# A fixed instruction order for TensorE in two chunked recurrences

## The chip, the core and the metric

The kernel runs on one core of one Trainium2 chip. The metric is the device time of one execution in microseconds; the profile beside it is that of one execution on the chip. TensorE (PE) multiplies matrices into PSUM, VectorE (DVE), ScalarE (ACT) and GpSimd (POOL) do the elementwise work, SyncE (SP) issues transfers.

## What is computed

One layer of a streaming encoder: a normalised and modulated input `h`, one input projection, two recurrences side by side (GLA with 4 heads of 64 x 128, HGRN2 with 4 heads of 128 x 128), a gated norm, and an output projection with a residual. 4096 prompt frames and 64 sample frames, width 1024. The recurrence of each head is

```
S_t = diag(exp g_t) S_{t-1} + k_t^T v_t,    o_t = q_t S_t
```

```python
h = rms_norm(x, g_pre) * (1 + scale[:, None]) + shift[:, None]
p = jnp.einsum('btd,de->bte', h, w_in)
q_a, k_a, v_a, z_a, a_lr, q_h, f_h, i_h, z_h = jnp.split(p, ...)
o_a, s_a = chunked_gla(q_a * GLA_DK ** -0.5, k_a, v_a, log_alpha, s_gla)
o_h, s_h = chunked_gla(silu(q_h), 1 - f, i_h, log(f), s_hgrn)
...
y = x + gate[:, None] * rms_norm(o, g_post)
```

Any evaluation of the recurrence that gives these values will do; the chunk size is free.

## The kernel before

The prompt is cut into 16 groups of 256 tokens (two tiles of 128); the 64 sample tokens ride as a third tile with the last group in GLA and with group 2 in HGRN. The kernel walks over the groups three times: GLA, HGRN, and a last pass with the output projection. Each projection is split into a high and a low part, three matmuls for each product.

**Main and sides.** In both recurrences a group's projection is a generator (`proj_gla`, `proj_hgrn`), and `weave` runs other generators beside it. The projection yields after every four and eight of its eight contraction steps (`proj_feat`, features by tokens, 12 matmuls of 256 columns a half; `proj_tok`, tokens by features, 12 matmuls of 264 or 512 columns a half). At each yield `weave` takes as many steps of each side as are due. Sides are: the `attend` of the group before, the preparation of the next group's input (`prep_x` in GLA, `prep_h` in HGRN), weights, and `gate_rows`. For a side `(gen, n, first, last)`, n steps are spread evenly over the yields `first` to `last`. A GLA group has 20 yields (four features of q and k, four z blocks, two v tiles), an HGRN group 20 as well (four f and four q features, two tiles of i).

**The order on the engines.** What the program traces is not yet the order in which an engine runs. A planner orders each engine's instructions with modelled times, by the order of the program as a priority and by what is ready; it also places tiles in the pools' buffers and adds every wait. TensorE's order is therefore the planner's. Only the first group's setup (`first_group`) stands in a block that keeps program order.

**The steps of an attend** (line 642), as `attend` yields. The first is taken right after the projection (`next(side)`), the other twelve beside the next group's projection:
1. nothing
2. transposes of A (L686), sums and products on VectorE
3. half as many transposes of A
4. transposes of A again
5. the first Y, and 6. the second Y (`prepare`, L911)
7. and 8. the score matmuls L956 on the Y's, `place` (L923) and `times`. GLA has two pairs of blocks, both in step 7; HGRN has four, two in step 7 and two in step 8
9. and 10. the levels 5 and 6 (L766)
11. and 12. the chunks: keys transposed (L793), A times v (L818), Q times S (L823), the state's increment (L839), the state's update (L850), the norm

The score part of `three_levels` (line 884), with pr running over the pairs of blocks:

```python
        ys = [prepare(0)]
        yield
        if NP > 1:
            ys.append(prepare(1))
        yield
        for pr in range(NP):
            ...
            Yt = ys.pop(0)
            ...
            if pr + 2 < NP:
                ys.append(prepare(pr + 2))
            if pr % 2 or pr == NP - 1:
                ...
```

Between `Yt = ys.pop(0)` and the next `prepare` stand the matmuls L956 of one pair (16 records in HGRN, 32 in GLA), which read Yt and K. `prepare` takes a tile from the pool `wstage`, which has two buffers: a whole one (`stage_pair`) for 128-token chunks, a half of one (`wst`, which cuts a pair and keeps the unused half in `self.halves`) for the 64-token set. Weights are staged in halves of the same pool. A Y is filled by a memset on GpSimd (L915), a copy on ScalarE (L916) and six products on VectorE, each of which reads the one before (L909).

**The input's norm in GLA.** From group 2 on, `quad_norm` (line 502) takes eight squares on ScalarE (L514), a small matmul with `same` (L517), a root, and a product; `x_turn` (line 522) transposes x on VectorE in four steps, modulates it into `hf`, and stores `hf` to `h_d`, where HGRN reads it again. `split_h` splits `hf` into the two parts `hh` that the next projection reads.

Of the kernel before, what the change touches and what calls it, by code (L numbers as in the profile page):

```python
# [15 lines left out]
P = 128  # L16
# [6 lines left out]
C_QA, C_VA, C_ZA, C_AL, C_QH, C_FH, C_IH, C_ZH = 0, 512, 1024, 1536, 1552, 2064, 2576, 3088  # L23
NMASK = 8
END = 20
LEVELS = 1


class Kernel:
# [472 lines left out]
    def quad_norm(self, g, js):  # L502

        nc = self.nc
        ss = self.small.tile([P, 8], F32, name="q_ss")
        n = 0
        tiles = []
        for j in js:
            nb = self.groups[g][j][2] // 32
            xv = self.xs[j][:, : nb * 256].rearrange("p (b f) -> p b f", b=nb)  # L510
            tiles.append((xv, n, nb))
            for b in range(nb):
                junk = self.ap.tile([P, 256], mybir.dt.bfloat16, name="sqx", bufs=1)
                nc.scalar.activation(junk, xv[:, b], AF.Square, accum_out=ss[:, n : n + 1])  # L514
                n += 1
        pt = self.ps("tp")[:, :n]
        nc.tensor.matmul(pt, self.same, ss[:, :n], start=True, stop=True)  # L517
        rs = self.rstd(pt, D, table=True)
        for xv, o, nb in tiles:
            nc.vector.tensor_tensor(xv, xv, rs[:, o : o + nb].unsqueeze(2).to_broadcast([P, nb, 256]), ALU.mult)  # L520

    def x_turn(self, g):

        nc = self.nc
        tl = self.groups[g]
        T = self.tokens(tl)
        self.hf = hf = [self.hp.tile([P, 2, T], F32, name="hf", bufs=4) for _ in range(4)]
        for tiles, cnd in (([0, 1], 0), ([2], 1)):
            if tiles[0] >= len(tl):
                continue  # L530
            if tiles[0] == 2:
                self.x_load(g, [2])
                self.quad_norm(g, [2])
            o0 = tl[tiles[0]][3]
            width = sum(tl[j][2] for j in tiles)
            if g < 2:
                for i in range(4):
                    pt = self.ps("tp").rearrange("p (k c) -> p k c", k=2)
                    for k in range(2 * i, 2 * i + 2):
                        for j in tiles:  # L540
                            nc.tensor.transpose(
                                pt[:, k % 2, j * P : (j + 1) * P], self.xs[j][:, k * P : (k + 1) * P], self.ident
                            )
                    for k in range(2 * i, 2 * i + 2):
                        dst, sc, bi = hf[i][:, k % 2], self.gs[:, k, cnd : cnd + 1], self.sh[:, k, cnd : cnd + 1]
                        if k % 2 == 0:
                            nc.scalar.activation(dst, pt[:, k % 2], AF.Identity, bias=bi, scale=sc)
                        else:
                            nc.vector.tensor_scalar(dst, pt[:, k % 2], sc, bi, ALU.mult, ALU.add)
                    yield  # L550
                continue
            for i in range(4):
                for j in tiles:
                    _, _, r, o = tl[j]
                    xv = self.xs[j][:, : r * 8].rearrange("p (b k i) -> p b k i", k=KT, i=32)
                    nc.vector.transpose(
                        hf[i][:, :, o : o + r].rearrange("p k (b t) -> p b k t", t=32), xv[:, :, 2 * i : 2 * i + 2]
                    )
                for k in range(2 * i, 2 * i + 2):
                    dst = hf[i][:, k % 2, o0 : o0 + width]  # L560
                    sc, bi = self.gs[:, k, cnd : cnd + 1], self.sh[:, k, cnd : cnd + 1]
                    if k % 2 == 0:
                        nc.scalar.activation(dst, dst, AF.Identity, bias=bi, scale=sc)
                    else:
                        nc.vector.tensor_scalar(dst, dst, sc, bi, ALU.mult, ALU.add)
                yield
        for i in range(4):
            nc.sync.dma_start(self.h_d[g][:, 2 * i : 2 * i + 2, :], hf[i][:, :, :GROUP])
            if len(tl) == 3:
                nc.sync.dma_start(self.h_s[:, 2 * i : 2 * i + 2, :], hf[i][:, :, GROUP:])  # L570
# [28 lines left out]
    def proj_feat(self, ps, W, c0, h, T):  # L599

        n = 3 * KT
        i = 0
        for kt in range(KT):
            hi, lo = [h(kt)[:, i, :] for i in range(2)]
            wh, wl = W[kt][:, 0, c0 : c0 + P], W[kt][:, 1, c0 : c0 + P]
            for a, b in ((wh, hi), (wh, lo), (wl, hi)):
                self.nc.tensor.matmul(ps[:, :T], a, b, start=i == 0, stop=i == n - 1)  # L607
                i += 1
            if kt == 3:
                yield  # L610

# [22 lines left out]
    def proj_tok(self, ps, W, c0, c1, h, o, r):  # L634

        for kt in range(KT):
            self.tok_step(ps, W, c0, c1, h(kt), o, r, kt)
            if kt == 3:
                yield

# [710 lines left out]
                    nc.sync.dma_start(dst[0, r0 : r0 + r, :], y[:r])  # L1351


    @staticmethod
    def weave(main, sides):

        sides = [[*s, 0] for s in sides if s[0] is not None]
        res = None  # L1360
        m = 0
        while True:
            try:
                next(main)
            except StopIteration as e:
                res = e.value
                break
            m += 1
            for s in sides:
                gen, n, first, last, done = s  # L1370
                while s[4] * (last - first) < n * (m - first):
                    s[4] += 1
                    next(gen, None)
        for s in sides:
            if s[3] < END:
                for _ in s[0]:
                    pass
        return res

    def run(self):  # L1380
# [5 lines left out]
        def now(gen):  # L1386
            for _ in gen:
                pass
# [3 lines left out]
        with ExitStack() as rec:  # L1392
# [6 lines left out]
            side = None  # L1399

            def prep_x(g):
                if g > 1:
                    self.x_load(g, [0, 1])
                (self.x_norm if g < 2 else self.quad_norm)(g, [0, 1])
                for _ in range(3):
                    yield
                yield from self.x_turn(g)

            def prep_h(g, tl):
                self.load_hf(g, tl)  # L1410
                yield

            for g in range(ng):
                prep = prep_x(g + 1) if g + 1 < ng else prep_h(0, self.groups2[0])
                sides = [(side, 12, 1, 18), (prep, 8, 0, 16) if g == 0 else (prep, 8, 7, 19)]
                if g == ng - 1:

                    sides.append((self.weights(W2["f"], C_FH, 512, "wu"), 10, 8, 18))
                    sides.append((self.weights(W2["q"], C_QH, 512, "wv"), 10, 20, 26))
                res = self.weave(self.proj_gla(g, h), sides)  # L1420
                h = self.split_h()
                side = self.attend_group(g, S, Ss, res, 2, 2, self.oa_d, t["new_gla_p"], t["new_gla_s"])
                next(side)
            S, Ss = [None], [t["state_hgrn"]]
            gate = self.gate_rows()
            per_gate = -(-28 // max(1, ng - self.beside - 2))
            for g in range(ng):
                prep = prep_h(g + 1, self.groups2[g + 1]) if g + 1 < ng else prep_h(0, self.groups2[0])
                sides = [
                    (side, 15 if g == 0 else 16 if g == self.beside + 1 else 12, 1, 18), (prep, 1, 4, 8),  # L1430
                    (gate if g > self.beside + 1 else None, per_gate, 0, END),
                ]
                if g == 0:
                    sides.append((self.weights(W2["i"], C_IH, 512, "wu"), 10, 0, 14))
                if g == ng - 1:
                    sides.append((self.weights(W3["z"], C_ZH, 512, "wu"), 10, 8, 18))
                res = self.weave(self.proj_hgrn(g, h), sides)
                h = self.split_h()
                side = self.attend_group(g, S, Ss, res, 4, 1, self.oh_d, t["new_hgrn_p"], t["new_hgrn_s"])
                next(side)  # L1440
            now(gate)
            tiles = [(g, j, tl) for g in range(ng) for j, tl in enumerate(self.groups2[g])]
            self.zq = []
# [17 lines left out]
            def until(n):  # L1461
                while len(self.zq) < n:
                    next(zg)
                    yield

            og = self.xp.tile([P, D], F32, name="xt", bufs=2)
            self.og_load(tiles[0], og)
            self.weave(until(4), [(side, 15, 0, 12), (self.load_wout(W3["o"]), 18, 0, 12)])

        def zone():  # L1470
            while True:
# [69 lines left out]
```

## Time and profile before

| | us |
|---|---|
| median of 3 runs (lowest, highest) | 2157.05 (2156.89, 2158.09) |
| the profiled execution | 2154.41 |
| its span, first to last instruction | 2152.6 |
| VectorE busy | 1492.5 |
| ScalarE busy | 996.1 |

The page cuts the span into 40 equal slices; the digits are busy shares in tenths. GLA takes about the first 14 slices, HGRN the next 15, the last pass the rest:

```profile
PE   8999999999999999999999999999989999999998
PEld 6888989889898888989999898999868888888887
DVE  6777767777677787677788777677995454545444
ACT  6666655665556664444444444444542222222212
POOL 3200010001100111110111111000330000000000
PEclk9999999999999999999999999999999999999999
```

PE is the busy share of matmuls, PEld that of weight loads, which overlap them; PEclk is the granted clock of TensorE. A matmul on 32-bit operands in the recurrence shows as two records. In a timeline the columns are start, duration, engine, line, operation, names, shapes, count, and in brackets the idle time before it and what ended it.

### The profile page before, as it was taken

What the parts mean: (1) busy time and instruction counts of PE and PEld (TensorE: products, weight loads), DVE (VectorE), ACT (ScalarE), POOL (GpSimd) and SP (SyncE); (2) the same over time, 40 slices, a digit from 0 to 9 for tenths busy, and PEclk for the clock granted to TensorE, in tenths of its full rate; (3) what the DMA queues carried; (4) which work ended last, traced back from release to release, by engine and by line L of the source; (5) the groups of instructions that cost most, each with busy time, mean ns of one, the idle gap of its engine ahead of it and who ended that gap; (6) DMA issues with size and microseconds to landing.
All of it is one profiled execution on the core that took longest, in us unless ns stands there. A gap on an engine that the chain in (4) does not pass through costs nothing.

```text
span 2152.6 us, 44904 instructions
## 1 busy us (share of the span) xinstructions
PE 2108.6 (98%) x16574; PEld 1849.9 (86%) x16574; DVE 1492.5 (69%) x4851; ACT 996.1 (46%) x2960; POOL 239.8 (11%) x640
## 2 busy tenths in 40 slices
PE   8999999999999999999999999999989999999998
PEld 6888989889898888989999898999868888888887
DVE  6777767777677787677788777677995454545444
ACT  6666655665556664444444444444542222222212
POOL 3200010001100111110111111000330000000000
PEclk9999999999999999999999999999999999999999
DMA  9322222222222321112211111011343333333322
GB/s 274 102 63 71 61 56 50 72 66 58 55 50 64 118 87 39 38 33 71 66 50 50 31 31 50 31 31 48 98 150 132 118 123 108 127 117 131 108 100 88
DMA packets 218632, 173.22 MB, mean 80 GB/s; under 512 B 136236, under 2 KB 158224, under 8 KB 218412
## 3 DMA queue, kind: packets, MB, share of 16 engines
q1 hardware_dynamic: 218268, 170.08, 26.8%
q8 instruction: 131, 2.15, 0.4%
q14 instruction: 89, 0.73, 0.1%
q10 hardware_dynamic: 144, 0.26, 0.0%
HBM read 118.35 MB, written 51.93 MB: 79 GB/s over the span
## 4 chain that ended last, share of the span: by engine, by line
PE 85%; DVE 8%; ACT 4%; issue 1%; DMA 1%; POOL 0%; SPq 0%; DVEq 0%; ACTq 0%; POOLq 0%
PE ps_pj L619 23%; PE ps_pj L607 22%; PE ps_pj L1335 16%; PE ps_at L619 7%; PE ps_at L686 2%; PE ps_ms L839 2%; PE ps_o L823 2%; PE ps_o L818 2%; PE ps_at L956 2%; PE ps_at L766 1%; DVE wst L909 1%; PE ps_tp L793 1%; ACT A L776 1%; PE ps_tp L1300 1%; PE ps_ms L1300 1%
## 5 line engine op out<-in xcount | busy, mean ns | idle before, releaser
L619 PE MATMUL ps_pj<-wu,hh 128*128 128x512 f32 x1632 | 410.7, 398 | 4.3 <-DVE hh L93 3.4
L607 PE MATMUL ps_pj<-hh,wu 128*128 128x256 f32 (+1 forms) x2976 | 392.3, 287 | 0.0
L607 PEld LDWEIGHTS ps_pj<-hh,wu 128*128 128x128 f32 x2976 | 372.9, 191 | 4.9 <-issue 0.3
L619 PEld LDWEIGHTS ps_pj<-wu,hh 128*128 128x128 f32 x1632 | 296.4, 188 | 66.0 <-DVE hh L93 3.9
L607 PE MATMUL ps_pj<-hh,wv 128*128 128x256 f32 (+1 forms) x1536 | 214.1, 289 | 0.0
L607 PEld LDWEIGHTS ps_pj<-hh,wv 128*128 128x128 f32 x1536 | 192.5, 188 | 14.9 <-issue 12.9
L619 PE MATMUL ps_pj<-wv,hh 128*128 128x264 f32 x1464 | 199.3, 290 | 1.9 <-DVE wv L93 1.9
L619 PEld LDWEIGHTS ps_pj<-wv,hh 128*128 128x128 f32 x1464 | 184.2, 188 | 7.1 <-issue 2.3
L1340 ACT ACTIVATE sq<-ps_pj 128x512 bf16<-128x512 f32 (+1 forms) x66 | 39.4, 597 | 294.7 <-PE ps_pj L1335 293.2
L1335 PE MATMUL ps_pj<-wv,ogh 128*128 128x512 f32 x512 | 162.2, 397 | 0.0
L1335 PE MATMUL ps_pj<-wu,ogh 128*128 128x512 f32 x512 | 158.0, 390 | 0.0
L619 PE MATMUL ps_at<-wu,hh 128*128 128x512 f32 x672 | 157.4, 390 | 0.0
L92 ACT CAST hh<-hf 128x512 fp32r<-128x512 f32 (+1 forms) x188 | 117.3, 626 | 68.6 <-PE ps_pj L619 37.0
L619 PEld LDWEIGHTS ps_at<-wu,hh 128*128 128x128 f32 x672 | 126.0, 188 | 26.1
L1201 ACT ACTIVATE g<-ps_pj 128x256 f32<-128x256 f32 (+1 forms) x128 | 49.4, 386 | 200.2 <-PE ps_pj L607 199.8
L93 DVE TENSOR_TENSOR hh<-hf,hh 128x512 fp32r<-128x512 f32 (+1 forms) x188 | 132.5, 711 | 6.5 <-ACT hh L92 5.5
L909 DVE TENSOR_TENSOR wst<-wst,T 128x160 f32<-128x160 f32 (+4 forms) x480 | 118.4, 265 | 4.0
L1335 PEld LDWEIGHTS ps_pj<-wu,ogh 128*128 128x128 f32 x512 | 96.1, 188 | 20.8
L938 POOL COPY T<-T 128x16 f32<-128x16 f32 (+1 forms) x32 | 9.9, 309 | 931.4 <-DVE Qg L879 827.8
L1335 PEld LDWEIGHTS ps_pj<-wv,ogh 128*128 128x128 f32 x512 | 93.8, 188 | 19.1
L1335 PE MATMUL ps_pj<-wv,ogl 128*128 128x512 f32 x256 | 100.5, 393 | 0.0
L1335 PE MATMUL ps_pj<-wu,ogl 128*128 128x512 f32 x256 | 99.7, 390 | 0.0
(303 smaller groups left out, 3758.5 us busy)
## 6 DMA issues: line engine op xcount, KB each, us to landing
hf<-h_d SPq DMA_DIRECT2D x128, 256.0 KB
xt<-in_x_prompt_dram SPq DMA_DIRECT2D x36, 512.0 KB
h_d<-hf SPq DMA_DIRECT2D x64, 256.0 KB
out_y_prompt_dram<-y SPq DMA_DIRECT2D x31, 512.0 KB
xt<-in_x_prompt_dram SPq DMA_DIRECT2D x448, 32.0 KB
wst<-in_w_in_dram SPq DMA_DIRECT2D x36, 256.0 KB
ada_st<-in_w_ada_dram SPq DMA_DIRECT2D x32, 256.0 KB
oa_d<-e SPq DMA_DIRECT2D x32, 256.0 KB
```

The costliest lines, as they stand in the source:

```text
L92: self.nc.scalar.copy(hi, src)
L93: (eng or self.nc.vector).tensor_tensor(lo, src, hi.bitcast(F32), ALU.subtract)
L607: self.nc.tensor.matmul(ps[:, :T], a, b, start=i == 0, stop=i == n - 1)
L619: self.nc.tensor.matmul(ps[:r, : c1 - c0], a, b, start=kt == 0 and i == 0, stop=kt == KT - 1 and i == 2)
L686: nc.tensor.transpose(pt[:, i * P : (i + 1) * P], D[:, c + i, :], self.ident)
L818: nc.tensor.matmul(po[h], A[:, c * 4 + h, :], v, start=h < n, stop=St is None and h == 4 - n)
L823: nc.tensor.matmul(o, Q[rows[s], c * G + g, :], St[rows[s], g, :], start=NS == 2 and not apart and h == 1, stop=h == 4 - NS or h == 3 and ...
L839: nc.tensor.matmul(pd[s * w : (s + 1) * w, g, :], kc[:CL, g, s * w : (s + 1) * w], vs[c][:CL, h * P : (h + 1) * P], start=not apart, stop= ...
L909: nc.vector.tensor_tensor(parts(dst), parts(src), t.unsqueeze(3).to_broadcast(shape), ALU.mult)
L956: nc.tensor.matmul(pas[s][rows, g0 + g], K[rr, 2 * pr + g, rows], Yt[rr, o : o + P], start=True, stop=True)
L1201: nc.scalar.activation(sg, pf[:, :T], AF.Sigmoid)
L1335: nc.tensor.matmul(po[:r], a[:, kt, :r], b, start=m == 0, stop=m == 3 * KT - 1)
```

## The change

- All TensorE instructions from GLA's first group to HGRN's last keep the order of the program; the other engines stay with the planner.
- `weave` counts the columns that the projection has streamed in the group (`self.work`, 32 added for each matmul). A side may now have a list of due points in thousands of columns instead of an even spread; its next step is taken at the first yield of the projection at which the point is passed. A GLA group streams 82 thousand, an HGRN group 81 thousand.
- Three lists: the attend beside a GLA projection, the attend beside an HGRN projection, and the input's preparation in GLA. The attends in the HGRN groups 0 and 3 keep an even spread, as do weights, gate rows and `prep_h`.
- `quad_norm` yields after the squares of each of its two tiles, so they stand at two points and the small matmul at a third.

```diff
+SIDE_GLA = [3, 9, 13, 19, 22, 28, 36, 40, 47, 54, 58, 64]
+SIDE_HGRN = [3, 9, 13, 19, 22, 27, 37, 46, 54, 61, 67, 72]
+PREP = [27, 31, 38, 45, 52, 58, 66, 72]
...
                 nc.scalar.activation(junk, xv[:, b], AF.Square, accum_out=ss[:, n : n + 1])
                 n += 1
+            yield
         pt = self.ps("tp")[:, :n]
...
                 self.nc.tensor.matmul(ps[:, :T], a, b, start=i == 0, stop=i == n - 1)
                 i += 1
+            self.work += 3 * (T + 32)
             if kt == 3:
                 yield
...
             self.tok_step(ps, W, c0, c1, h(kt), o, r, kt)
+            self.work += (2 if r < P else 3) * (c1 - c0 + 32)
...
-                gen, n, first, last, done = s
-                while s[4] * (last - first) < n * (m - first):
-                    s[4] += 1
+                gen, due, done = s
+                if isinstance(due, list):
+                    while s[2] < len(due) and 1000 * due[s[2]] <= self.work:
+                        s[2] += 1
+                        next(gen, None)
+                    continue
+                n, first, last = due
+                while s[2] * (last - first) < n * (m - first):
+                    s[2] += 1
                     next(gen, None)
...
-                (self.x_norm if g < 2 else self.quad_norm)(g, [0, 1])
-                for _ in range(3):
+                    yield from self.quad_norm(g, [0, 1])
+                else:
+                    self.x_norm(g, [0, 1])
+                    yield
                     yield
+                yield
                 yield from self.x_turn(g)
...
+            tensor = rec.enter_context(ExitStack())
+            tensor.enter_context(self.tc.manual_schedule(engines={mybir.EngineType.PE}))
             for g in range(ng):
...
-                sides = [(side, 12, 1, 18), (prep, 8, 0, 16) if g == 0 else (prep, 8, 7, 19)]
+                sides = [(side, SIDE_GLA), (prep, (8, 0, 16) if g == 0 else PREP)]
...
-                    (side, 15 if g == 0 else 16 if g == self.beside + 1 else 12, 1, 18), (prep, 1, 4, 8),
-                    (gate if g > self.beside + 1 else None, per_gate, 0, END),
+                    (side, (15, 1, 18) if g == 0 else (16, 1, 18) if g == self.beside + 1 else SIDE_HGRN),
+                    (prep, (1, 4, 8)), (gate if g > self.beside + 1 else None, (per_gate, 0, END)),
...
                 next(side)
+            tensor.close()
             now(gate)
```

More of the change, by code (lines that the diff above doesn't have):

```diff
@@ L532, in x_turn @@
                 self.x_load(g, [2])
-                self.quad_norm(g, [2])
+                for _ in self.quad_norm(g, [2]):
+                    pass
             o0 = tl[tiles[0]][3]
@@ L1351, in phase3, with weave @@
                     nc.sync.dma_start(dst[0, r0 : r0 + r, :], y[:r])
-    @staticmethod
-    def weave(main, sides):
+    def weave(self, main, sides):
         sides = [[*s, 0] for s in sides if s[0] is not None]
@@ L1361, in weave @@
         m = 0
+        self.work = 0
         while True:
@@ L1369, in weave @@
             for s in sides:
-                gen, n, first, last, done = s
-                while s[4] * (last - first) < n * (m - first):
-                    s[4] += 1
+                gen, due, done = s
[7 more added lines that the diff above has]
+                    s[2] += 1
                     next(gen, None)
-        for s in sides:
-            if s[3] < END:
-                for _ in s[0]:
+        for gen, due, _ in sides:
+            if isinstance(due, list) or due[2] < END:
+                for _ in gen:
                     pass
@@ L1411, in prep_h @@
                 yield
+            tensor = rec.enter_context(ExitStack())
+            tensor.enter_context(self.tc.manual_schedule(engines={mybir.EngineType.PE}))
             for g in range(ng):
                 prep = prep_x(g + 1) if g + 1 < ng else prep_h(0, self.groups2[0])
-                sides = [(side, 12, 1, 18), (prep, 8, 0, 16) if g == 0 else (prep, 8, 7, 19)]
+                sides = [(side, SIDE_GLA), (prep, (8, 0, 16) if g == 0 else PREP)]
                 if g == ng - 1:
-                    sides.append((self.weights(W2["f"], C_FH, 512, "wu"), 10, 8, 18))
-                    sides.append((self.weights(W2["q"], C_QH, 512, "wv"), 10, 20, 26))
+                    sides.append((self.weights(W2["f"], C_FH, 512, "wu"), (10, 8, 18)))
+                    sides.append((self.weights(W2["q"], C_QH, 512, "wv"), (10, 20, 26)))
                 res = self.weave(self.proj_gla(g, h), sides)
@@ L1429, in run @@
                 sides = [
-                    (side, 15 if g == 0 else 16 if g == self.beside + 1 else 12, 1, 18), (prep, 1, 4, 8),
-                    (gate if g > self.beside + 1 else None, per_gate, 0, END),
+                    (side, (15, 1, 18) if g == 0 else (16, 1, 18) if g == self.beside + 1 else SIDE_HGRN),
+                    (prep, (1, 4, 8)), (gate if g > self.beside + 1 else None, (per_gate, 0, END)),
                 ]
                 if g == 0:
-                    sides.append((self.weights(W2["i"], C_IH, 512, "wu"), 10, 0, 14))
+                    sides.append((self.weights(W2["i"], C_IH, 512, "wu"), (10, 0, 14)))
                 if g == ng - 1:
-                    sides.append((self.weights(W3["z"], C_ZH, 512, "wu"), 10, 8, 18))
+                    sides.append((self.weights(W3["z"], C_ZH, 512, "wu"), (10, 8, 18)))
                 res = self.weave(self.proj_hgrn(g, h), sides)
@@ L1467, in run @@
             self.og_load(tiles[0], og)
-            self.weave(until(4), [(side, 15, 0, 12), (self.load_wout(W3["o"]), 18, 0, 12)])
+            self.weave(until(4), [(side, (15, 0, 12)), (self.load_wout(W3["o"]), (18, 0, 12))])
         def zone():
```

## The prediction, made before the result was seen

> **What bounds the kernel now.** I read the head of the page first, then the chain that ended last, then the busy times of two long stretches: the GLA recurrence without its first groups, and the HGRN recurrence.
>
> ```profile
> span 2152.6 us, 44904 instructions
> PE 2108.6 (98%) x16574; PEld 1849.9 (86%) x16574; DVE 1492.5 (69%) x4851; ACT 996.1 (46%) x2960; POOL 239.8 (11%) x640
> PE 85%; DVE 8%; ACT 4%; issue 1%; DMA 1%; POOL 0%; SPq 0%; DVEq 0%; ACTq 0%; POOLq 0%
> 120.00:705.00 585.00, 577.40 (x5487) 522.77 (x5486) 431.11 (x1502) 356.45 (x1276) 62.56 (x208) 1.00 0.26 62
> 752.00:1555.00 803.00, 796.24 (x7065) 717.61 (x7063) 624.02 (x2153) 379.27 (x1079) 113.78 (x333) 1.00 0.16 50
> ```
>
> TensorE is the bound: 98% of the span, 577.4 of 585 us in the one stretch, 796.2 of 803 us in the other, at a granted clock of 1.00. VectorE comes second with 624 of 803 us. Whatever lets TensorE stand longer lengthens the time one for one; only what makes it stand less can shorten it. So the next view is what it waits for: the waits of PE, first in 120 to 705 us (one row), then in 800 to 1555 us (two rows; total, times, longest).
>
> ```profile
> PE ps_tp L517 <- ACT sqx L514: 6.6, 11, 0.8
> ...
> PE ps_at L766 <- DVE K L909: 2.2, 11, 0.3
> PE ps_at L956 <- DVE wst L909: 0.7, 3, 0.3
> ```
>
> In GLA there is one wait worth naming, the norm's small product on the squares, 6.6 us in all. In HGRN waits come to some 3 us. The order that the planner found for TensorE leaves little to win.
>
> **What is gained.** First the squares (L514, L517). The timeline of one GLA group:
>
> ```profile
> 455.59 0.85 PE L956 MATMUL ps_at<-wst,K 64*32 64x128 f32 x36
> ...
> 455.97 0.41 ACT L514 ACTIVATE sqx<-xt 128x256 bf16<-128x256 f32 x1
> 456.98 0.19 ACT L514 ACTIVATION_READ_ACCUMULATOR sqx<-xt 128x1 f32 x1
> ...
> 457.22 0.39 PE L517 MATMUL ps_tp<-q_ss,same 128*128 128x8 f32 x2 [0.78 <-ACT sqx L514]
> 457.54 0.65 PE L956 MATMUL ps_at<-wst,K 64*32 64x128 f32 x28
> ```
>
> The planner put L517 into the middle of the score matmuls, 0.78 us ahead of its last square. After the change the squares are traced at 27 and 31 thousand columns, L517 at 38, behind all 64 scores. From the later squares to L517 TensorE has 24 z matmuls of 264 columns and the scores to do, over 3 us, and four squares take ScalarE some 2.3 us (1.2 for the two from 455.97 to 457.17, with other work between). I take the whole 6.6 us; if ScalarE is still late they stay. The x loads and the h_d stores move with their steps, on SP's queue, which TensorE reaches only through hf a stage later: I cost them at nothing. The last transposing step of x moves from 62 to 69 thousand columns, still a v tile of 24 matmuls ahead of the group's end.
>
> Second, interruptions of the projection. Two stretches of 24 matmuls, the first uninterrupted, the second behind a block of transposes:
>
> ```profile
> 1169.41 3.03 PE L607 MATMUL ps_pj<-hh,wu 128*128 128x256 f32 x24
> 1172.28 1.03 PE L686 MATMUL ps_at<-ident,A 128*128 128x128 f32 x8
> ...
> 1174.95 3.12 PE L607 MATMUL ps_pj<-hh,wu 128*128 128x256 f32 x24
> 1177.91 1.04 PE L686 MATMUL ps_at<-ident,A 128*128 128x128 f32 x8
> ```
>
> From start to the next start 2.87 against 2.96 us: an interruption by transposes costs 0.09 us. At 0.1196 us each, 20 such matmuls need 2.39 us; between two score blocks (1185.62 to 1188.28, below) they take 2.66: 0.27 us. In TensorE's timeline of the GLA group from 434.7 to 479.6 us I count 12 interruptions; after the change there are 8 (three of transposes, scores with L517, L1070 with the first L766, second L766, chunk 0, L1098 with chunk 1). Four fewer at 0.09 to 0.27, taken at 0.12 because they are mostly of the cheap kind: 0.5 us. In that of the HGRN group from 1167.5 to 1216.4 us there are 12 without the gate's; after, 9. Those that go are score blocks and half an L766: 3 x 0.27 = 0.8 us. Over 15 groups each: 7.5 and 12 us. **Gain 6.6 + 7.5 + 12 = 26 us** (16 with all at 0.09, 35 with all at 0.27).
>
> **What is lost.** Program order fixes something that the planner had moved. In `three_levels` the matmuls of pair 0 and pair 1 stand in one step, with nothing of TensorE between them; so do those of pairs 2 and 3. Each pair reads its own tile Y (name wst), which six chained L909 on VectorE fill. The timeline of one HGRN group:
>
> ```profile
> 1185.04 0.64 PE L956 MATMUL ps_at<-wst,K 128*32 128x128 f32 x16
> ...
> 1185.62 2.66 PE L607 MATMUL ps_pj<-hh,wv 128*128 128x256 f32 x20
> 1185.78 0.38 ACT L916 COPY wst<-Qg 128x224 f32<-128x224 f32 x1 [0.25 <-PE ps_at L956]
> ...
> 1185.91 0.35 DVE L909 TENSOR_TENSOR wst<-Qg,T 128x192 f32<-128x192 f32 x1
> 1186.29 0.33 DVE L909 TENSOR_TENSOR wst<-wst,T 128x160 f32<-128x160 f32 x1
> 1186.53 0.62 DVE L909 TENSOR_TENSOR Qg<-Qg,T 128x448 f32<-128x448 f32 x1
> 1187.07 1.06 DVE L909 TENSOR_TENSOR wst<-wst,T 128x128 f32<-128x128 f32 x4
> ...
> 1188.28 0.65 PE L956 MATMUL ps_at<-wst,K 128*32 128x128 f32 x16
> 1188.85 2.64 PE L607 MATMUL ps_pj<-hh,wv 128*128 128x256 f32 x20
> 1189.01 0.36 DVE L909 TENSOR_TENSOR wst<-Qg,T 128x192 f32<-128x192 f32 x1 [0.87 <-PE ps_at L956]
> ...
> 1190.77 0.19 DVE L909 TENSOR_TENSOR wst<-wst,T 128x32 f32<-128x32 f32 x1
> ...
> 1191.99 1.22 PE L607 MATMUL ps_pj<-hh,wv 128*128 128x256 f32 x8
> ...
> 1195.42 0.64 PE L956 MATMUL ps_at<-wst,K 128*32 128x128 f32 x16
> ```
>
> Filling a Y starts only when the scores on the Y before it are done: the copy at 1185.78 was released by L956, the next fill at 1189.01 too. So in HGRN one Y is alive at a time, though the pool has two buffers. The waits between 820 and 1500 us say the same of the whole stage:
>
> ```profile
> POOL wst L915 <- PE ps_at L956: 135.9, 56, 4.9
> ACT wst L916 <- PE ps_at L956: 71.5, 42, 3.1
> ...
> 447.55 0.66 ACT L916 COPY wst<-Qg 128x224 f32<-128x224 f32 x2 [0.78 <-DVE dd L730]
> ```
>
> The last row is GLA: two Y's filled together, eight us ahead of their scores. The code explains the difference: `wst()` hands out halves of the same buffers, the 64-token set of GLA takes one half, and its other half is popped only groups later; from then on an odd half always holds a buffer. The change touches none of this. So it adds a wait for Y in front of pairs 1 and 3, and behind it on TensorE stand the scores and the whole rest of the projection, hence everything.
>
> Its price: before, the planner filled these waits with 20 projection matmuls. Pair 0's block ends at 1185.62 for the next instruction, pair 1 starts at 1188.28: **2.66 us**. Without the 0.62 us on Qg in between, the chain is that of the next pair: 1188.85 to 1190.96, and 0.15 us from the last L909 to the matmul: 2.26 us. For pair 3 the interval is 1191.99 to 1195.42, 3.43 us, with a gate row's addition in it; I take 2.8, between 2.26 and 3.43, nearer to the rows without it. Sum 5.46 us a group. HGRN's weaves carry an attend of HGRN in 15 groups (the last runs beside the z tiles, outside): **15 x 5.46 = 82 us** (68 to 91).
>
> The other stages I hold to be covered. Pairs 2 and 3 come 36 matmuls, 4.3 us, behind pairs 0 and 1, and pair 2's fill needs 2.3. L766 follows pair 3 by 24 matmuls, 2.9 us; before, its first half waited 0.7 us. Chunk 1 ends 12 matmuls ahead of the group's end, so the buffer A comes free later, but the transposes that use it next stand 36 matmuls into the next group. The two weaves that keep even positions (groups 0 and 3) may wait more: 0 to 10 us, at the upper end only.
>
> **The clock.** TensorE's long gaps in the trace, and the granted clock behind them (in the rows that begin with a stretch, the first pair is PE's busy time and count, the third number from the end the granted clock):
>
> ```profile
> 24.26 0.50 PE L619 MATMUL ps_pj<-wv,hh 128*128 128x264 f32 x2 [1.90 <-DVE wv L93]
> 21.28:24.69 3.41, 1.51 (x11) 1.16 (x10) 3.41 (x4) 0.18 (x1) 2.35 (x1) 1.00 1.21 303
> 24.69:28.10 3.41, 3.41 (x17) 3.01 (x16) 2.61 (x8) 2.30 (x4) 0.00 (x0) 0.50 1.13 329
> ...
> 1556.53 1.47 PE L619 MATMUL ps_pj<-wu,hh 128*128 128x512 f32 x4 [3.44 <-DVE hh L93]
> 1558.00:1559.00 1.00, 1.00 (x7) 1.00 (x6) 1.00 (x3) 0.00 (x0) 0.00 (x0) 0.50 0.72 205
> ...
> 1611.90:1615.30 3.40, 1.62 (x9) 1.44 (x10) 2.91 (x6) 1.79 (x3) 0.00 (x0) 1.00 0.91 284
> 1615.30:1618.70 3.40, 3.40 (x18) 2.81 (x17) 1.29 (x3) 0.69 (x1) 0.00 (x0) 1.00 0.89 310
> ```
>
> A stretch of 3.41 us with 1.51 us of work was followed by 3.41 us at half clock; one with 1.62 us of work was not. A gap of 2.66 us leaves 0.75 us of work where it falls wholly into such a stretch, so it can halve the clock for 3.41 us, at a cost of 1.7 us. Whether it does hangs on where the stretches begin: at the 1.51 us of the row, 1.9 us of the gap must lie in one, which is (1.5 + 0.75)/3.41, two in three; at none of 30 is the other bound. I take one in three: **10 x 1.7 = 17 us** (0 to 34).
>
> The Trainium skill, page "TensorE: Matmul & The Clock Gate", section "HAM oscillation — how this bites in real kernels", states that only idle gaps of more than about 3.4 us bring the clock down. By that the term is nothing and the sum 17 us lower. The trace doesn't agree: its first drop follows a gap of 1.90 us at the longest.
>
> **The sum.** Against the profiled execution's own 2154.4 us (its span 2152.6 and 1.8 around it): 2154.4 - 26 + 82 + 17 = 2227. The median of the runs shown is 2.6 us over that execution, so 2229 in their terms.
>
> **The rivals.**
> - The clock holds through all gaps: 2157 - 26 + 82 = 2213. For it: 1611.90 to 1615.30 above. Against it: 21.28 to 24.69. Chance 0.26.
> - More waits than counted, all stalls at their long end, two in three of them with a clock drop, the even weaves late: 2157 - 16 + 91 + 34 + 4 = 2270. VectorE's 78% in HGRN speaks for it. 0.08.
> - The wait for Y doesn't come about: two Y's are alive in HGRN, as in GLA. Then only the gain is left: 2157 - 26 = 2131, faster. It decides at the fill of pair 1: if L916 for it runs ahead of pair 0's scores, this case holds. Against it stand the 56 and 42 waits above, and that nothing in the change hands a buffer back. 0.12. That TensorE isn't really in program order would come out between this and no change; it is in the next figure.
> - Within 0.2%, with one stall covered and the other paid for by the gain: 0.02.
>
> My forecast, stall and some clock drops, has the remaining 0.52.
>
> **How the numbers follow.** 0.2% of the time, 4.3 us, is about what a measurement of this kernel can tell from no change. Slower: 0.52 + 0.26 + 0.08 = 0.86; same 0.02; faster 0.12. The slow cases run from 2157 - 35 + 68 = 2190 to about 2270; that range leaves out the faster case and a little of each tail, so I give 2190 to 2270.
>
> **What would show it.** Right: the waits of PE in HGRN list L956 on DVE wst L909 some 30 times for about 80 us; the two score blocks of a step stand 2.3 to 3.4 us apart with no L607 between; HGRN's period grows by 4 to 6 us a group; some slices of HGRN show a clock below 9. L517's wait is gone and GLA's groups are about 1 us shorter. Wrong: two L916 side by side in HGRN, or L956 blocks that follow one another at once; then the time falls by 20 to 30 us. If the clock stays at 9 throughout, the third term is off and the rest holds.

## The result and the profile after

The change made the kernel slower, by far more than forecast: 2286.0 us (median of 4 executions, 2284.6 to 2288.7) against 2157.6 us (4 executions; the 2157.05 above is the median of the first three), a ratio of 1.0597, 95% interval 1.0578 to 1.0615. I had forecast 2229 us and a range up to 2270: 72 us more than before, where 128 came.

In the rows of the changed kernel the line numbers are 5 to 8 higher: L522 was L517 (the small product on the squares), L613 and L626 are the projection's matmuls (L607, L619), L694 the transposes of A (L686), L801 the keys' transposes (L793), L917 the six products that fill a Y (L909), L964 the score matmuls (L956), L1078 was L1070. The head of the page, two of its rows of 40 slices, and the chain that ended last by engine:

```profile
span 2283.5 us, 44875 instructions
PE 2130.3 (93%) x16574; PEld 1876.3 (82%) x16574; DVE 1501.7 (66%) x4851; ACT 999.2 (44%) x2960; POOL 233.1 (10%) x640
PE   8799999999999989889999988998998999999998
PEclk9999999999999999989999999999999999999999
PE 72%; DVE 17%; ACT 5%; issue 3%; DMA 1%; SPq 1%; DVEq 0%; POOL 0%; ACTq 0%; POOLq 0%
```

TensorE has as many matmuls as before (16574) and is busy 22 us longer, while the span grew by 131: most of the loss is standing still, a part is slower work. VectorE's share of the chain went from 8% to 17%: TensorE now waits for it. The clock's digits hardly move, because a drop of 3.4 us is lost in a slice of 57; they are the wrong view for this question. The waits of PE (total, times, longest):

```profile
PE ps_at L964 <- DVE wst L917: 80.7, 32, 2.9
PE ps_ms L1078 <- DVE at L1073: 10.4, 2, 9.2
PE ps_tp L522 <- ACT sqx L518: 9.5, 13, 6.3
PE ps_tp L801 <- DVE K L886: 7.8, 13, 0.6
PE ps_at L694 <- DVE dd L700: 5.7, 9, 1.7
```

The first row is the predicted wait for tile Y, nearly to the number (82 us, some 30 times). The other four, 33 us together, weren't predicted; L522's, 6.6 us before, had been expected to go. The timeline of one HGRN group shows the first row at work:

```profile
1047.66 0.64 PE L964 MATMUL ps_at<-wst,K 128*32 128x128 f32 x16
1050.78 1.08 PE L964 MATMUL ps_at<-wst,K 128*32 128x128 f32 x16 [2.47 <-DVE wst L917]
1051.79 5.54 PE L613 MATMUL ps_pj<-hh,wv 128*128 128x256 f32 x36
1057.27 0.64 PE L964 MATMUL ps_at<-wst,K 128*32 128x128 f32 x16
1060.63 0.91 PE L964 MATMUL ps_at<-wst,K 128*32 128x128 f32 x16 [2.72 <-DVE wst L917]
```

Between the two pairs of a step stands nothing, where the planner had put 20 projection matmuls. And the 16 scores behind a wait take 1.08 and 0.91 us in place of 0.64: the clock. One slice of HGRN shows an 8, as the prediction had given for a sign.

**Where the 131 us are.** I cut both traces at the first feature matmul of each group's projection, so that each piece is nearly one weave (the planner may move work over the cut), and compared them piece by piece (us; the group number is that of the projection, the attend in it belongs to the group before):

```
                              after - before   of it foreseen
setup and GLA group 0              +10.0              0
GLA group 1                         +6.6           -0.9
GLA groups 2 to 13                  -3.7          -11.3
GLA groups 14 and 15                +7.2           -1.9
HGRN group 0                        +8.2              0
HGRN group 3                       +14.4           +5.8
HGRN groups 1, 2, 4 to 14          +86.9          +75.4
HGRN group 15, all behind it        +1.2           +5.8
sum                               +130.8          +72.9
```

HGRN's group 15 goes by the list too, but its end can't be told from the last pass here. The foreseen column spreads the forecast's three terms evenly: 14.1 us of gain over 15 GLA groups, and (82 + 17 - 12)/15 for each of 15 HGRN groups. The 13 HGRN groups whose attend goes by the list are only a fifth of the miss; the rest lies at the seams (the start, GLA's last groups, HGRN's groups 0 and 3) and in GLA.

### The profile page after: what moved, and what is told of

It reads as the page before. It is cut to its first block, busy times and chain, and to the rows that moved or that the text cites. A ratio compares the mean times of both kernels' runs of the same rounds, so it can differ in the third digit from the quotient of the medians.

```text
span 2283.5 us, 44875 instructions
## 1 busy us (share of the span) xinstructions
PE 2130.3 (93%) x16574; PEld 1876.3 (82%) x16574; DVE 1501.7 (66%) x4851; ACT 999.2 (44%) x2960; POOL 233.1 (10%) x640
## 4 chain that ended last, share of the span: by engine, by line
PE 72%; DVE 17%; ACT 5%; issue 3%; DMA 1%; SPq 1%; DVEq 0%; POOL 0%; ACTq 0%; POOLq 0%
PE ps_pj L613 22%; PE ps_pj L626 16%; PE ps_pj L1343 15%; PE ps_at L626 6%; DVE wst L917 2%; PE ps_at L694 2%; PE ps_at L964 2%; PE ps_o L831 2%; DVE hh L97 1%; PE ps_o L826 1%; PE ps_ms L847 1%; PE ps_at L774 1%; ACT sqx L518 1%; ACT sq L866 1%; SPq L490 1%
## 5 line engine op out<-in xcount | busy, mean ns | idle before, releaser
L626 PE MATMUL ps_pj<-wu,hh 128*128 128x512 f32 x1632 | 405.4, 399 | 0.7 <-ACT v L1130 0.7
L613 PE MATMUL ps_pj<-hh,wu 128*128 128x256 f32 (+1 forms) x2976 | 393.8, 288 | 3.4 <-ACT hh L96 3.0
L613 PEld LDWEIGHTS ps_pj<-hh,wu 128*128 128x128 f32 x2976 | 375.3, 192 | 8.4 <-ACT hh L96 3.4
L626 PEld LDWEIGHTS ps_pj<-wu,hh 128*128 128x128 f32 x1632 | 299.1, 189 | 65.2 <-issue 3.2
L613 PE MATMUL ps_pj<-hh,wv 128*128 128x256 f32 (+1 forms) x1536 | 226.3, 311 | 0.0
L613 PEld LDWEIGHTS ps_pj<-hh,wv 128*128 128x128 f32 x1536 | 217.3, 215 | 8.9 <-issue 7.7
L626 PE MATMUL ps_pj<-wv,hh 128*128 128x264 f32 x1464 | 193.2, 289 | 2.9 <-DVE wv L97 1.9
L626 PEld LDWEIGHTS ps_pj<-wv,hh 128*128 128x128 f32 x1464 | 183.7, 191 | 4.2 <-DVE wv L97 2.1
L626 PE MATMUL ps_at<-wu,hh 128*128 128x512 f32 x672 | 158.4, 391 | 0.2 <-ACT A L784 0.2
L626 PEld LDWEIGHTS ps_at<-wu,hh 128*128 128x128 f32 x672 | 126.7, 189 | 26.7 <-ACT A L784 0.5
L964 PE MATMUL ps_at<-wst,K 64*32 64x128 f32 (+1 forms) x2048 | 63.5, 286 | 79.5 <-DVE wst L917 78.9
L917 DVE TENSOR_TENSOR wst<-wst,T 128x160 f32<-128x160 f32 (+4 forms) x480 | 118.9, 263 | 5.0
L964 PEld LDWEIGHTS ps_at<-wst,K 64*32 64x32 f32 (+1 forms) x2048 | 41.1, 110 | 94.9 <-issue 85.1
L941 ACT ACTIVATE A<-Ac,member 128x128 f32<-128x128 f32 x256 | 80.2, 389 | 87.9 <-DVE Ac L935 87.9
```

The costliest lines, as they stand in the source:

```text
L626: self.nc.tensor.matmul(ps[:r, : c1 - c0], a, b, start=kt == 0 and i == 0, stop=kt == KT - 1 and i == 2)
L917: nc.vector.tensor_tensor(parts(dst), parts(src), t.unsqueeze(3).to_broadcast(shape), ALU.mult)
L941: nc.scalar.activation(Ah[:, :, 32 * b : 32 * b + 32], Ach, AF.Copy, scale=self.member[:CL, 8 + b : 9 + b])
L964: nc.tensor.matmul(pas[s][rows, g0 + g], K[rr, 2 * pr + g, rows], Yt[rr, o : o + P], start=True, stop=True)
```

## The experiments

My theory after the result: the wait for Y makes some 80 us and the clock drops behind it 37 to 39, and at the seams the fixed order waits for whatever the planner had moved out of the way. The rivals: the loss is the lists' placing of the steps, not the fixed order; or the clock has no part in it; or VectorE bounds the scores in program order, whatever the number of Y's. All ratios are to the kernel before on the same chip, with 95% intervals. In the windows' rows stand the stretch, its length, the busy times (counts) of PE, PEld, DVE, ACT and POOL, PE's granted clock, DMA's share, and GB/s. The stretch is always HGRN's groups 4 to 14; the first two rows are those of the kernel before and of the changed one:

```profile
974.01:1503.67 529.66, 527.22 (x4742) 478.16 (x4740) 406.81 (x1394) 240.04 (x676) 65.18 (x198) 1.00 0.14 43
```

```profile
1029.62:1633.25 603.63, 542.97 (x4742) 495.18 (x4740) 412.06 (x1375) 239.56 (x676) 63.86 (x198) 0.96 0.11 36
```

The same 4742 matmuls take 74.0 us longer, of which TensorE stands 58.2 more (603.63 - 542.97 against 529.66 - 527.22) and works 15.8 more, at a mean clock of 0.96.

### Two Y's alive (e1_two_y)

```diff
-            Yt = self.stage_pair() if B == 4 else self.wst()
+            Yt = self.stage_pair() if B == 4 else self.stage_pair()[:, :528]
```

The 64-token set takes a whole buffer as well, so that no odd half keeps one.

> The changed kernel with two tiles Y alive in HGRN: the 64-token set takes a whole pair from the pool instead of a half, so no odd half holds a buffer. Theory (one Y in program order makes TensorE wait, and the waits halve the clock): the waits of PE for L917 (80.7 us, 32 times) nearly vanish, and with them some 39 us of the slow clock in HGRN (78 us at half clock); 2286 - 80 - 39 + 5 for waits that show up behind = about 2170, an HGRN group from 54.8 to about 47.5 us, clock 1.00 in the steady groups. Rival (VectorE, at two thirds of the span busy, is what bounds the scores in program order): the waits move to the scores of pairs 2 and 3, at least half of the loss stays, 2225 or more.

Measured: 2192.5 us, ratio 1.0171 (1.0154 to 1.0188). The scores in the timeline and the wait for Y, then the row of the 11 groups:

```profile
1131.67 1.13 PE L964 MATMUL ps_at<-wst,K 128*32 128x128 f32 x32
1132.73 4.54 PE L613 MATMUL ps_pj<-hh,wv 128*128 128x256 f32 x36
```

```profile
PE ps_at L964 <- DVE wst L917: 15.2, 5, 7.5
```

```profile
1018.38:1538.01 519.63, 516.38 (x4742) 475.57 (x4740) 403.99 (x1375) 235.82 (x676) 62.92 (x198) 1.00 0.14 42
```

Two pairs follow one another as 32 matmuls without a gap, the clock stays at 1.00, and the 11 groups take 10.0 us less than in the kernel before. So one line gives back 94 us, and in these groups the fixed order then beats the planner's. The time came out 22 us over the 2170 expected: what is left against before, 35 us in the spans, lies at the seams: 15.4 in the setup and GLA's groups 0 and 1, 8.4 in GLA's 14 and 15, 13.4 and 13.7 in HGRN's 0 and 3, together 51, of which the other pieces give 16 back. Two terms of the expectation were off: 15.2 us of waits for Y stayed, and of the slow clock some 29 us went in place of 39 (mean granted clock 0.974 over 2283.5 us, then 0.986 over 2187.3). The five remaining waits are in HGRN's groups 0 (7.5 us), 3 and 15, none in the 13 list groups compared above.

### The gap filled, the wait kept (e2_fill)

```diff
-                pas = [self.ps("at").rearrange("p (h c) -> p h c", h=4) for _ in range(NS)]
+                raw = [self.ps("at") for _ in range(NS)]
+                pas = [a.rearrange("p (h c) -> p h c", h=4) for a in raw]
             Yt = ys.pop(0)
+            if pr % 2 and NP == 4:
+                for _ in range(20):
+                    nc.tensor.matmul(raw[0][:, 256:], self.wal[:, :P], self.wal, start=True, stop=True)
```

Here 20 matmuls that nothing reads, of the shape 80x128 by 80x256, are added ahead of pairs 1 and 3; they write to an unused half of a bank.

> The changed kernel with 20 more matmuls (80x128 on 80x256, on constants, results overwritten) in front of the scores of pairs 1 and 3 of each 128-token HGRN attend, where TensorE stands still; still one Y. Theory (waits and clock are two separate costs; the clock falls because TensorE idles for more than about half of a 3.41 us stretch): pair 1 still starts when its Y is filled, so a group keeps its 5.2 us, but the clock stays at 1.00 in the steady groups; 24 drops in HGRN less 2 in the first groups, 1.7 us each: 2286 - 37 = about 2249. Rival (the slow stretches cost little, since TensorE waits for VectorE anyway): 2281 to 2290.

Measured: 2262.0 us, ratio 1.0486 (1.0471 to 1.0502), 24 us off the changed kernel. The two pairs of a step, and the 11 groups:

```profile
1147.75 0.65 PE L968 MATMUL ps_at<-wst,K 128*32 128x128 f32 x16
1148.32 2.66 PE L961 MATMUL ps_at<-wal 80*128 80x256 f32 x20
1150.91 0.64 PE L968 MATMUL ps_at<-wst,K 128*32 128x128 f32 x16
```

```profile
1023.45:1605.53 582.08, 576.95 (x5181) 528.86 (x5180) 412.33 (x1375) 237.25 (x676) 64.34 (x198) 1.00 0.12 38
```

The useless work takes the place of the wait and saves nothing of it, but the scores behind it take 0.64 us again and the clock is back at 1.00: 21.5 us less in the 11 groups, which had 15 stretches at half clock in the changed kernel. So a drop costs 1.4 us, and the clock is a term of its own, apart from the wait. The theory had 37 us for 22 drops at 1.7; in the 13 list groups 26.0 came, from 18 drops. That the clock has no part falls; that it is all of it falls too, since 62.4 us remain against two Y's (582.08 - 519.63).

### The lists without the fixed order (e3_planner)

```diff
-            tensor.enter_context(self.tc.manual_schedule(engines={mybir.EngineType.PE}))
```

> The changed kernel without the fixed order of TensorE: due points, column counts and the split squares stay, the planner orders TensorE again. Theory (the fixed order alone makes the loss): 2157 plus or minus 8, no wait for L917 over 3 us in all, no drop of the clock in HGRN. Rival (the later stages by the lists make part of the loss): 2180 or more.

Measured: 2158.5 us, ratio 1.0005 (0.9996 to 1.0015). The lists and the split squares are worth nothing together; the fixed order makes the loss. But the pieces show that this nothing is a sum: GLA's groups 2 to 13 gain 8.4 us, more than the 3.7 under the fixed order, while the 13 list groups of HGRN lose 7.1, group 14 of GLA 3.8, and the setup with group 0 3.3 (the control below has 2.7 there with nothing changed in it, so that this much isn't the lists'). In GLA the reason can be read. First the changed kernel, then this one, one steady group each:

```profile
695.58 0.39 PE L522 MATMUL ps_tp<-q_ss,same 128*128 128x8 f32 x2 [0.26 <-ACT sqx L518]
708.03 0.44 PE L801 MATMUL ps_tp<-ident,K 128*128 128x128 f32 x2 [0.60 <-DVE K L886]
```

```profile
412.60 0.39 PE L522 MATMUL ps_tp<-q_ss,same 128*128 128x8 f32 x2 [0.55 <-ACT sqx L518]
425.04 0.44 PE L801 MATMUL ps_tp<-ident,K 128*128 128x128 f32 x2
```

With the planner's order L522 waits longer, but the keys' transposes wait for nothing: the planner takes other matmuls first. In program order they stand right where they were traced and wait 0.60 us a group.

### The fixed order from GLA's third group on (e4_late)

```diff
-            tensor.enter_context(self.tc.manual_schedule(engines={mybir.EngineType.PE}))
             for g in range(ng):
+                if g == 2:
+                    tensor.enter_context(self.tc.manual_schedule(engines={mybir.EngineType.PE}))
```

> The changed kernel with the fixed order from GLA's group 2 on instead of group 0. Theory (16.6 us of the loss come from the first two weaves: 9.2 us in which the gate's transposes L1078 wait ahead of the v tiles, 6.35 us on the first strided x load, and four slow stretches of the clock): 2286 - 16 = about 2270. Rival (the wait on the first x load only moves into group 2, since the planner no longer hides it there either): 2277 or more.

Measured: 2274.4 us, ratio 1.0547 (1.0531 to 1.0563), 11.6 us off the changed kernel and 4 short of the theory. What the fixed order did at the start is seen in the timelines, of the kernel before first, then of the changed one:

```profile
66.51 3.83 PE L619 MATMUL ps_pj<-wu,hh 128*128 128x512 f32 x16
71.22 3.92 PE L619 MATMUL ps_pj<-wu,hh 128*128 128x512 f32 x16 [0.87 <-ACT K L1036]
...
112.77 0.28 PE L517 MATMUL ps_tp<-q_ss,same 128*128 128x8 f32 x2
```

```profile
75.37 0.96 PE L1078 MATMUL ps_ms<-ident,at 128*80 128x128 f32 x2 [9.24 <-DVE at L1073]
...
116.51 0.60 PE L522 MATMUL ps_tp<-q_ss,same 128*128 128x8 f32 x2 [6.35 <-ACT sqx L518]
```

The planner had put 32 v matmuls ahead of the small transpose L1070, and in group 1 the squares' product among the first v matmuls, behind all of z. In program order TensorE stands 9.24 and 6.35 us at these two places. Without the fixed order in groups 0 and 1 both waits go, but one comes back in the first group that has it:

```profile
153.52 0.59 PE L522 MATMUL ps_tp<-q_ss,same 128*128 128x8 f32 x2 [6.08 <-ACT sqx L518]
```

So this seam moved with the edge of the block. What stands behind it is mainly SP's queue. In group 1 of the changed kernel (start, duration, queue or engine, line, names, count):

```profile
99.87 13.27 SPq L490 DMA_DIRECT2D xt<-in_x_prompt_dram  x19
114.19 0.40 ACT L518 ACTIVATE sqx<-xt 128x256 bf16<-128x256 f32 x1
```

The loads of x leave the queue one after another, 0.70 us each on average, until 113.1, and the last four squares start from 114.19 on, long after the scores ended at 110.2. The last load landed at 114.7, by its semaphore in the trace, so most of the 6.35 us is the loads'. Not all of it: ScalarE also has seven activations of the attend (L941) ahead of these squares, from 112.14 on.

### A second Y under the planner, a control (c1_before_two_y)

The line of the first experiment in the kernel before.

> The kernel before with a whole tile for every Y, so that two can be alive in HGRN; the planner keeps TensorE's order. Theory: the planner fills every wait for a Y with projection anyway, so a second Y alone is worth nothing: 2157 us, 4 either way. Rival: the second Y itself is worth something, and part of what the second Y brought in the changed kernel (94 us) is no wait of the fixed order: 6 us faster or more.

Measured: 2154.5 us, ratio 0.9991 (0.9983 to 1.0). Within the 4 us of the theory: the second Y is worth nothing to a planner that fills the gap, and 94 us to a fixed order that can't. It even costs HGRN's group 0 2.2 us (a wait of 2.31 us and a clock drop).

### One Y, with the pairs in steps of their own (e6_apart)

```diff
-SIDE_HGRN = [3, 9, 13, 19, 22, 27, 37, 46, 54, 61, 67, 72]
+SIDE_HGRN = [3, 9, 13, 19, 22, 27, 34, 41, 48, 55, 61, 68, 74, 80]
...
         for pr in range(NP):
             ...
+            if NP == 4 and pr % 2 == 0:
+                yield
             if pr % 2 or pr == NP - 1:
```

> The changed kernel, with one Y alive as it is, but with the four pairs of HGRN's scores in four steps at 27, 34, 41 and 48 thousand columns, so that 24 projection matmuls (2.9 us) stand between two pairs; the later steps follow at 55, 61, 68, 74 and 80. Theory: what costs is that nothing stands between two scores that share a Y, so nearly all of the 81 us of waits and of the clock drops behind them go: 2175 to 2195 us, as with two Y's (2192.5). Rival: it is the number of Y's that counts, or the later steps run over the end of the group and wait there: 2215 us or more.

Measured: 2207.9 us, ratio 1.0237 (1.0223 to 1.0251). Two neighbouring pairs, the wait for Y, and the 11 groups:

```profile
1140.25 0.64 PE L964 MATMUL ps_at<-wst,K 128*32 128x128 f32 x16
1140.82 0.64 PE L446 MATMUL ps_tp<-e,c 128*4 128x512 f32 x2
1141.30 3.02 PE L613 MATMUL ps_pj<-hh,wv 128*128 128x256 f32 x24
1144.24 0.64 PE L964 MATMUL ps_at<-wst,K 128*32 128x128 f32 x16
```

```profile
PE ps_at L964 <- DVE wst L917: 18.5, 13, 2.9
```

```profile
1016.87:1552.05 535.18, 524.05 (x4742) 474.33 (x4740) 406.63 (x1368) 236.89 (x669) 74.39 (x198) 1.00 0.13 41
```

The tile is still one, and yet 62 of 81 us of waits and all clock drops of the list groups are gone; 68.5 of the 74.0 us in the 11 groups come back. So the place of the scores is what costs, and the number of Y's only decides whether the place matters. The time lies between theory (up to 2195) and rival (2215): the groups 5 to 10, in which the gate rows run, keep a wait of 1.1 to 1.5 us each at L964, and the seams and the last pass make another 53 us.

### The fixed order only where it gains (e5_steady)

Two Y's, and in HGRN the block opened and closed around each group; all of GLA is left to the planner:

```diff
-            tensor.enter_context(self.tc.manual_schedule(engines={mybir.EngineType.PE}))
...
             for g in range(ng):
+                tensor.close()
+                if g in (1, 2, *range(4, ng)):
+                    tensor.enter_context(self.tc.manual_schedule(engines={mybir.EngineType.PE}))
```

> The changed kernel with two Y's alive, and TensorE's fixed order only in the 14 HGRN groups whose attend goes by the list (all but 0 and 3). Theory: such a group gains about 1.0 us (47.8 against 48.83 us in the profiles of the changed kernel with two Y's and of the kernel before), and the start, GLA's end and the even weaves cost nothing under the planner: 2157 - 13 = 2144 us, 4 either way. Rival: each entry into the fixed order brings waits of its own, as GLA's third group did when the order began there (11.6 us off the start became 6 us of a wait and a clock drop): 2157 us or more.

Measured: 2142.6 us, ratio 0.9936 (0.9922 to 0.995): 0.6% below the kernel before, and faster than the changed one. The 11 groups:

```profile
968.85:1488.31 519.46, 516.47 (x4742) 475.47 (x4741) 404.29 (x1375) 235.83 (x676) 62.73 (x198) 1.00 0.14 44
```

The total is as expected, but its parts are not quite: the 13 list groups give 12.2 us, GLA's groups 2 to 13 another 8.4 by their lists, and group 14 of GLA (3.8) and group 0 of HGRN (3.4) take back nearly as much. I had taken all of GLA for nothing.

### The fixed order in GLA too (e7_both)

As in the run above, with the block in GLA's groups 4 to 13 as well.

> As the run with the fixed order in 14 HGRN groups, and besides in the GLA groups 4 to 13. Theory: a steady GLA group gains 0.3 us (44.8 to 44.5 in the profiles), so 3 us more: 2141 us. Rival: the entry into GLA's fixed order brings one wait for the squares and the x load, 6 us and a clock drop: 2150 us or more.

Measured: 2149.9 us, ratio 0.9964 (0.9952 to 0.9977). Slower than without it, and for neither reason. There is no wait of 6 us at the entry: L522 waits 0.55 us there, because SP has issued the loads of x before the scores end; the entry cost of the run from group 2 on belongs to the first groups. But a GLA group takes 44.5 us in the fixed order and 44.1 under the planner with the same lists, since L801 waits 0.6 us again; I had compared with the 44.8 of the kernel before, whose lists were other ones. That is 4.1 us; the other 5.4 of the 9.5 us by which the spans differ lie nearly all in the setup and the last pass, which the edit doesn't touch.

### The last GLA group prepared evenly (e8_last)

The run with the block in 14 groups, and one spread changed:

```diff
-                sides = [(side, SIDE_GLA), (prep, (8, 0, 16) if g == 0 else PREP)]
+                sides = [(side, SIDE_GLA), (prep, (8, 0, 16) if g == 0 else (10, 7, 19) if g == ng - 2 else PREP)]
```

> As the run with the fixed order in 14 HGRN groups (2142.6 us), but the input of the last GLA group, the one with the sample tile, prepared by an even spread over the yields 7 to 19 of the group before it, as in the kernel before, in place of the list. Theory: the list takes the last steps of that preparation at 72 thousand columns, and the sample tile, normed after them, comes late: the group that prepares it takes 48.9 us in place of 45.1. So 3 to 4 us go: 2139 us. Rival: the loss is at the seam whatever the spread, since the planner moves transposes of the next group ahead of it: 2142 us, 2 either way.

Measured: 2145.1 us, ratio 0.9946 (0.9932 to 0.996). The theory falls, and the time is 3 us over the rival's 2142 too. Group 14 is back at 44.8 us from 48.9, but group 15 takes 63.2 in place of 57.2, 6.8 of them at half clock. Its first matmuls still wait 1.07 us for hh. The loss at this seam moves across the group's edge with the spread. What would remove it stays open.

## Why the prediction was wrong

- **The wait for Y**, the largest term, was right in mechanism, place, number and size: 82 us foreseen, 80.7 measured in 32 waits. Of these 68.1 us stand in 26 waits of the 13 list groups, for which the forecast has 71; the other six are in groups 0, 3 and 15. The two experiments that remove it by different ways (a second Y, a distance between pairs) and the control settle it.
- **The gain in HGRN** was right: 12 us foreseen for 15 groups; 12.9 measured with two Y's in 13. The mechanism holds as well: in groups 4 to 14 the projection is interrupted 110 times in place of 148, counted in the traces, and the same matmuls are busy 10.8 us less (527.22 against 516.38), 0.29 us for each interruption that went (0.27 foreseen).
- **The clock** was right as a mechanism and too small. Of the 26 waits in the 13 list groups 18 were followed by a stretch at half clock, not one in three. A drop costs 1.4 us (26.0 us between these groups of the changed kernel and those with the gap filled, over 18), not 1.7. For 15 groups this makes 30 us in place of 17, inside the bounds of 0 to 34; the working of the prediction had itself given two in three, and I chose the lower value without a reason. The rival in which the clock holds falls, and with it the rule named beside that term: the scores at 1050.78 and 1060.63 are slow behind gaps of 2.47 and 2.72 us.
- **"The other stages I hold to be covered"** is the step that failed, together with the start, which had no term at all: outside the two pairs of scores the cost of program order was put at nothing. The step was argued from the list groups, where it holds. The even weaves were set to 0 to 10 us, at the upper end only, and the upper case then carried 4 of it. They cost 8.2 us (group 0) and 14.4 (group 3). In group 3, by the trace, TensorE waits 7.0 us for Y and 3.9 at L694, and has half its clock for 13.7 us. With two Y's 4.3 us of the waits for Y stay, and the group is still 13.7 us over the kernel before; with two Y's under the planner it is 0.5 under. Group 0 is 0.3 over under the planner with one Y. So in these two it is the fixed order that costs, and a second Y doesn't help. Why group 3, whose attend has the sample tile beside it, still waits for Y with two of them stays open.
- **The start**, the other half of that step: the fixed order begins in the first group, and the long waits that the planner had covered there could have been looked for by putting the steps of GLA's groups 0 and 1 in program order. The start cost 16.6 us, two waits of 9.24 and 6.35 us among them (some 3 us of the setup vary from run to run, by the control). The second wait goes against a step of the prediction, that the x loads reach TensorE only through hf a stage later: they reach it in the same stage, through the squares and L522.
- **The gain in GLA** was too large: 14 us foreseen; 3.7 came in groups 2 to 13. L522 still waits 0.26 us, and a new wait of 0.6 at L801 took most of what the fewer interruptions (8 a group in place of 11 to 13) gave. Under the planner the same lists give 8.4.

Of the 58 us between forecast and result in the spans, the start and GLA's group 1 make 17.5, HGRN's groups 0 and 3 16.8, the list groups 11.5 (nearly all clock), GLA's last two groups 9.1 and the steady ones 7.6; HGRN's last group with the last pass gives 4.6 back. That GLA's last two groups lose by the lists and not by the order is only partly shown: 3.8 us of it is there under the planner too.

## What to carry to other kernels

A hand-fixed order costs wherever the planner had been filling a wait; so it pays only where every wait of the program order has been priced, and the seams (first groups, a group with an odd tile, the change from one loop to the next) must be priced one by one. Before an engine's order is fixed, look for the pairs of steps that share one buffer and stand side by side: give them a second buffer or some work in between. A fixed order can be limited to the groups where it wins: here that, with the second Y, turned 6% slower into 0.6% faster.

## What the hardware showed

Through GLA's steady groups and HGRN the clock of TensorE dropped by the share of idle time in a stretch of 3.41 us, not by the length of a gap. Windows of the changed kernel, cut where the trace changes the clock and 3.413 us on from there; first one with a drop, then a gap split over two stretches, last an exception in the setup:

```profile
1047.19:1050.60 3.41, 1.12 (x21) 0.72 (x19) 2.06 (x7) 0.38 (x1) 0.11 (x1) 1.00 0.00 0
1050.60:1054.02 3.42, 3.24 (x26) 2.89 (x27) 1.98 (x12) 0.38 (x1) 0.11 (x1) 0.50 0.00 0
1101.80:1105.21 3.41, 2.22 (x30) 1.81 (x29) 1.49 (x4) 0.76 (x2) 0.11 (x1) 1.00 0.25 77
1105.21:1108.63 3.42, 2.15 (x29) 1.98 (x30) 2.44 (x13) 0.38 (x1) 0.11 (x1) 1.00 0.02 5
1108.63:1112.04 3.41, 3.41 (x42) 3.15 (x40) 1.23 (x8) 2.05 (x6) 0.00 (x0) 1.00 0.00 0
12.97:16.39 3.42, 2.04 (x12) 1.22 (x13) 1.64 (x6) 3.16 (x6) 0.95 (x1) 1.00 1.05 313
16.39:19.80 3.41, 2.99 (x16) 1.52 (x15) 3.38 (x5) 3.41 (x8) 1.43 (x1) 0.50 1.16 309
```

With 1.12 us of work in a stretch the next has half the clock; the same gap of 2.47 us, cut in two by the edge of the stretches (2.22 and 2.15 us of work), costs nothing. I laid this grid over the whole trace: from 122 us on, among stretches at full clock, all 27 with an idle share of at least 0.56 were followed by half the clock, and none with 0.544 or less. The two stretches of the kernel before in the prediction, idle 0.557 and 0.524, fall on the same two sides. The border doesn't hold everywhere, though. In the setup a stretch with an idle share of 0.40 was followed by half the clock (12.97 to 16.39), as was one with 2.05 us of work in e8_last (699.45 to 702.87), while one with 1.45 us of work, idle 0.57, in e6_apart (1664.50 to 1667.91) was not. Stretches that were already at half clock don't follow it either (one with an idle share of 0.33 was followed by another). What counts besides the idle share stays open.

The Trainium skill, page "TensorE: Matmul & The Clock Gate", section "Part 1: The HAM clock gate", says that the clock goes by a free-running window of 3413 ns; the trace agrees, with half-clock stretches of 3.413 or 3.414 us or two to three times that. The rule of the same page's section "HAM oscillation — how this bites in real kernels", no idle gaps of more than about 3.4 us, isn't enough here: gaps of 2.47 and 2.72 us halved the clock.
